# A hybrid attention layer on one core: 72 TensorE transposes become 32x32 block transposes on VectorE, and the planner counts the pieces of transfers under way

## The chip, the core and the metric

The kernel runs on one core of a Trainium2 chip. The metric is the time of the whole program on the device in microseconds. One launch computes everything: a prompt of 1,024 tokens and a sample of 32 tokens, in float32.

The core's engines are TensorE (PE in the profile, with its weight loads as PEld), VectorE (DVE), ScalarE (ACT) and GpSimd (POOL). SyncE (SP) issues all transfers of this kernel, in the order of its instructions.

## The reference

One layer, applied to the prompt and to the sample with the same weights:

```python
hn = rmsnorm(h, g_pre)
qA, kA, vA, gA, qB, kB, vB, gB = split(hn @ w_in)       # eight times 512 columns
oA = band_attention(qA, kA, vA, rel_bias)               # 8 heads x 64, own chunk of 64 and 8 before
oB = stick_breaking(qB, kB, vB)                         # 8 heads x 64, strictly causal
y  = concat(oA * silu(gA), oB * silu(gB)) @ w_out
h  = h + rmsnorm(y, g_post)
h  = h + sigmoid(h @ w_ple_gate) * (p @ w_ple)
```

The sample's 32 queries also attend to 512 cached keys and values for each kind of attention. Besides the two results, the outputs are the new keys and values: those of kind A for the last 512 prompt tokens, those of kind B for all 1,024, and all of them for the 32 sample tokens.

## The kernel before

**Tiles.** The 1,024 + 32 tokens lie side by side as 1,056 columns in three blocks of 352 (`CH`). The normed input is kept transposed, features on the partitions, split into a high and a low float32r half (`hnh`, `hnl`), and every large product is the sum of three float32r products. `norm_tile` scales a tile of 128 tokens (`scale_x`), and `turn_x` transposes it, by eight transposes of 128x128 against the identity on TensorE into PSUM; ScalarE copies the high half from there, VectorE subtracts for the low half.

**Order of the program.** First the tiles of x are loaded, scaled and turned and the first pair's q, k and v are projected, block by block. Then come eight steps, one for each pair of heads, A and B in turn. In a step, `weave` interleaves the attention of this pair (`seq`: scores S, turned weights T, values V for each block of 128 queries) with the projections of the next pair (`den`); `RATE` sets the ratio in which it takes from the two, `SPACE_S`, `SPACE_T` and `SPACE_V` add to the weights of the attention's pieces. In the odd pairs the sample's attention for four heads (`sample_attention`: load, queries, scores, weights, values, out) is inserted at the positions `SAMPLE_AT`. In four steps, sums of quarters of w_out and w_ple_gate are made (`sum_weights`), at fixed positions. After that come the gates' projections, the product of p with w_ple (`class Ple`), and the two 1,024 x 1,024 products by Strassen-like blocks, which end the program.

**The planner.** No engine's order is the program's. `Recorder` records every operation with the operations that it depends on, and its `order` runs a list simulation: each engine has a time at which it is free, each operation a cost (`cost`), and of the operations that are ready the one with the smallest key `(class or low, number in the program)` goes next. A transfer occupies SyncE for `ISSUE` = 550 ns, moves after `DMA_NS` = 1500 ns, at `DMA_RATE` or a cost by pieces, and is taken to have landed `DMA_MARGIN` = 2000 ns later. All instructions come from one line of the recorder, so the profile gives the line 462 for each, and tiles and operations tell them apart.

**Buffers that the change touches.** The tag "tok" of `at2` has two buffers. Keys (`keys_out`), values before and after their turn (`values_out`), p_prompt's tiles (`load_p`) and the left sides of the last products rotate through them. The rings "om" and "be" hold the attention's rows and also tiles of x and the cached keys (`Kc`).

**Transposes before the change, other than the attention's weights.**
- K for its output: VectorE turns the prompt's columns in 32x32 blocks, and four stores, one for each group of 32 features, put them right in pieces of 128 bytes. The 32 sample tokens go through one TensorE transpose (`short_block`) and a copy.
- V, which the attention needs with tokens on the partitions: VectorE turns 32x32 blocks, a store to a scratch and four loads move whole blocks, and ScalarE orders them. The sample tokens go through `short_block` again.
- The sample's cached keys: a load of 128 tokens x 256 features four times, and eight TensorE transposes for each of the four sample attentions.
- The sample's outputs: the diagonal blocks of PSUM are copied to one tile, two TensorE transposes and a copy turn them, and two stores write them.
- p_prompt: two transposes for each tile of 128 tokens.

Of the kernel before, what the change touches and what calls it, by code (L numbers as in the profile page):

```python
# [13 lines left out]
P = 128  # L14
# [12 lines left out]
NT = 9  # L27

# [5 lines left out]
SPACE_S = 0.1  # L34
SPACE_T = 0.4
SPACE_V = 0.0
PARTS = 4
BEHIND = 2
RATE = 1.0
# [135 lines left out]
class Op:  # L175
    __slots__ = ("eng", "what", "args", "kw", "key", "busy", "late", "ready", "left", "after", "at", "size", "shared", "table")
# [7 lines left out]
DMA_NS, DMA_RATE, DMA_MARGIN = 1500, 320.0, 2000  # L184
# [81 lines left out]
class Recorder:  # L266
# [44 lines left out]
    def add(self, eng, what, args, kw):  # L311
# [29 lines left out]
        o.busy, o.late = self.cost(eng, method, args, kw, writes, reads)  # L341
        o.shared = eng == "POOL"
        if eng == "DVE":
            sbuf = [v for v in reads if isinstance(v, (View, Segments)) and not v.buf.psum and v.free() > 4]
            o.shared = len(sbuf) > 1 or (method == "tensor_copy" and len(sbuf) == 1 and not writes[0].buf.psum)

# [35 lines left out]
    def order(self):  # L382
# [16 lines left out]
        out, port, line, table = [], 0.0, 0.0, AF.Exp  # L399
        while len(out) < len(self.ops):  # L400
# [67 lines left out]
def stream_step(  # L468
# [27 lines left out]
    vs_dr = {ab: scratch([NS, 512], f"vs_dr{ab}") for ab in "AB"}  # L496
# [102 lines left out]

    def turn_x(t, sq, n):  # L600
        for kh in range(2):
# [105 lines left out]
    def values_out(ab, p, src, o_p, o_s, then):  # L707
# [5 lines left out]
        def turn():  # L713
# [27 lines left out]
    def col_steps(j):  # L741
# [67 lines left out]
    def attention(ab, p, h):  # L809
# [152 lines left out]
        for i in range(8):  # L962
            out["S", i] = (0.107 * cost(i) + SPACE_S, lambda i=i: scores(i))
            out["T", i] = (0.107 * cost(i) + SPACE_T, lambda i=i: weights_t(i))
        for g in range(2):
            columns = sum(reach(g, b).stop - reach(g, b).start for b in range(4 * g + 4))
            out["V", g] = (0.00088 * columns + SPACE_V, lambda g=g: values(g))
# [11 lines left out]
    def sample_attention(ab, gi):  # L979
# [19 lines left out]
        def queries():  # L999
# [25 lines left out]
        def scores():  # L1025
# [33 lines left out]
            dma(vn, vs_dr[ab][:, 256 * gi:256 * gi + 256])  # L1059
# [33 lines left out]
        def values():  # L1093
# [792 lines left out]
```

## Time and profile before

| | |
|---|---|
| time, median of 3 runs | 786.2 us (785.92 to 786.36) |
| span of the profiled execution | 784.8 us |
| TensorE busy | 776.3 us, 4,606 matmuls, clock 0.999 |
| VectorE, ScalarE, GpSimd busy | 582.2, 531.6, 475.1 us |
| DMA | 153.64 MB in 161,245 packets, of which 38,593 under 512 bytes |

The profile is of one execution; of that execution it gives the span, from its first to its last instruction, and no other time of its own. The span is 1.4 us under the median of the runs, and this difference is carried along. Instructions of an engine are counted busy from start to end, so overlapping matmuls have a longer mean duration than the step from one to the next.

### The profile page before, as it was taken

The page shows a single profiled execution, that of the slowest core. Times are in us where ns is not written, and L with a number is a line of the kernel's source. Part 1 is how long each engine was busy: PE and PEld are TensorE (multiplying, and loading weights), DVE is VectorE, ACT ScalarE, POOL GpSimd, SP SyncE. Part 2 cuts the span into 40 slices and gives each one's busy share as a digit, 9 for nine tenths or more (in the row PEclk, how much of TensorE's full clock was granted, in tenths as well). Part 3 has the DMA queues.
Part 4 walks back from the last instruction along what each step waited for, and adds up shares of the span by engine and source line. Part 5 has one row for each costly group of instructions (what it writes and reads, how often), then busy time and mean ns, then how long its engine had stood idle before and what let it go on. Part 6 is the DMA issues. An engine that isn't in the chain of part 4 may idle for free.

```text
span 784.8 us, 14442 instructions
## 1 busy us (share of the span) xinstructions
PE 776.3 (99%) x4606; PEld 718.1 (92%) x4606; DVE 582.2 (74%) x1106; ACT 531.6 (68%) x1171; POOL 475.1 (61%) x555
## 2 busy tenths in 40 slices
PE   8999999999999999999999999999999999999997
PEld 6999999999999999999999999999998787888786
DVE  7717577896788788786888688766565677989965
ACT  6647686786797677787776697753347967777651
POOL 5626534666585447775966586566553529599523
PEclk9999999999999999999999999999999999999999
DMA  9627634538774638776758767556589856859854
GB/s 304 214 82 190 144 91 133 154 82 257 202 198 138 174 96 248 191 230 190 202 167 244 186 212 236 169 170 186 145 272 309 271 171 204 285 167 342 276 161 134
DMA packets 161245, 153.64 MB, mean 196 GB/s; under 512 B 38593, under 2 KB 127337, under 8 KB 161170
## 3 DMA queue, kind: packets, MB, share of 16 engines
q1 hardware_dynamic: 161170, 152.73, 65.4%
q8 instruction: 36, 0.59, 0.3%
q14 instruction: 39, 0.32, 0.1%
HBM read 94.45 MB, written 49.83 MB: 184 GB/s over the span
## 4 chain that ended last, share of the span: by engine, by line
PE 94%; POOL 2%; DVE 1%; DMA 1%; issue 1%; SPq 0%; ACT 0%; DVEq 0%; ACTq 0%; POOLq 0%
PE mm_kB L462 6%; PE mm_vA L462 6%; PE mm_gA L462 6%; PE mm_qA L462 6%; PE mm_qB L462 6%; PE mm_gB L462 6%; PE mm_vB L462 5%; PE mm_kA L462 5%; PE SB L462 4%; PE PVB L462 4%; PE SA L462 4%; PE PVA L462 3%; PE ptwA L462 3%; PE ptwB L462 3%; PE g1P L462 2%; PE o3P L462 2%
## 5 line engine op out<-in xcount | busy, mean ns | idle before, releaser
L462 POOL TENSOR_TENSOR be<-be,om 128x256 f32<-128x256 f32 (+8 forms) x66 | 85.4, 1298 | 78.6 <-DVE om L462 31.3
L462 DVE TENSOR_TENSOR_SCAN om<-om,SB 128x384 f32<-128x384 f32 (+5 forms) x96 | 92.4, 967 | 20.2 <-ACT be L462 12.4
L462 POOL TENSOR_SCALAR be<-be,statA 128x640 f32<-128x640 f32 (+3 forms) x64 | 45.7, 719 | 44.5 <-DVE statA L462 33.4
L462 ACT ACTIVATE om<-SB 128x384 f32<-128x384 f32 (+5 forms) x96 | 46.8, 497 | 25.7 <-DVE SB L462 19.2
L462 ACT ACTIVATE be<-SB 128x384 f32<-128x384 f32 (+5 forms) x96 | 46.5, 498 | 9.3 <-DVE wTl L462 3.7
L462 ACT ACTIVATE be<-om,statA 128x640 f32<-128x640 f32 (+3 forms) x64 | 44.6, 698 | 11.5 <-DVE statA L462 5.9
L462 DVE TENSOR_TENSOR wTl<-ptwA,wTh 128x512 fp32r<-128x512 f32 (+2 forms) x80 | 37.5, 483 | 14.6 <-ACT wTh L462 13.8
L462 ACT CAST wTh<-ptwA 128x512 fp32r<-128x512 f32 (+2 forms) x80 | 32.6, 425 | 15.1 <-PE ptwA L462 14.1
L462 DVE TENSOR_TENSOR wTl<-ptwB,wTh 128x512 fp32r<-128x512 f32 (+3 forms) x64 | 33.9, 546 | 6.0 <-ACT wTh L462 5.6
L462 DVE CUSTOM_DVE_ANT_0 om<-SA,biasA 128x320 f32<-128x320 f32 (+3 forms) x64 | 30.2, 484 | 6.2 <-PE SA L462 5.5
L462 ACT CAST wTh<-ptwB 128x512 fp32r<-128x512 f32 (+3 forms) x64 | 29.4, 485 | 7.6 <-PE ptwB L462 7.0
L462 PE MATMUL SB<-kdB,LB 128*128 128x384 f32 (+5 forms) x96 | 33.6, 356 | 0.3 <-DVE LB L462 0.3
L462 PE MATMUL ptwA<-ident,be 128*128 128x128 f32 x200 | 33.4, 273 | 0.0
L462 PE MATMUL SB<-klB,LB 128*128 128x384 f32 (+5 forms) x96 | 32.8, 346 | 0.0
L462 DVE TENSOR_TENSOR wTl<-be,wTh 128x640 fp32r<-128x640 f32 (+1 forms) x24 | 29.7, 1237 | 3.2 <-ACT wTh L462 3.1
L462 PE MATMUL SA<-kdA,LA 128*128 128x320 f32 (+2 forms) x96 | 30.6, 322 | 0.0
L462 PE MATMUL SA<-klA,LA 128*128 128x320 f32 (+2 forms) x96 | 30.0, 313 | 0.0
L462 PE MATMUL ptwB<-ident,be 128*128 128x128 f32 x192 | 29.5, 273 | 0.0
L462 POOL TENSOR_TENSOR oB<-oB,oB 128x256 f32<-128x256 f32 x32 | 26.5, 853 | 3.9 <-DMA oB<-in_w_out_dram 3.9
L462 PEld LDWEIGHTS ptwA<-ident,be 128*128 128x128 f32 x200 | 24.8, 140 | 1.1
L462 POOL TENSOR_TENSOR klA<-stkA,kdA 64x1024 fp32r<-64x1024 f32 (+2 forms) x9 | 20.0, 2218 | 9.5 <-ACT kdA L462 9.2
L462 DVE STREAM_TRANSPOSE om<-be 128x640 f32<-128x640 f32 (+1 forms) x24 | 22.2, 925 | 4.6 <-POOL be L462 3.9
(711 smaller groups left out, 2676.7 us busy)
## 6 DMA issues: line engine op xcount, KB each, us to landing
oB<-in_w_out_dram SPq DMA_DIRECT2D x16, 256.0 KB, 4.2
sum_dro<-oB SPq DMA_DIRECT2D x16, 256.0 KB, 2.5
gB<-in_w_ple_gate_dram SPq DMA_DIRECT2D x16, 256.0 KB, 4.2
sum_drg<-gB SPq DMA_DIRECT2D x16, 256.0 KB, 2.3
x<-in_x_prompt_dram SPq DMA_DIRECT2D x16, 256.0 KB, 4.4
h_dr<-h SPq DMA_DIRECT2D x8, 512.0 KB, 4.1
ht<-h_dr SPq DMA_DIRECT2D x8, 512.0 KB, 4.1
raw<-sum_drg SPq DMA_DIRECT2D x16, 256.0 KB, 3.8
```

The source lines that it names most:

```text
L462: getattr(getattr(tc.nc, o.what[0]), o.what[1])(*args, **kw)
```

## The change

Five groups of transposes leave TensorE. Each is now done by VectorE in 32x32 blocks, and the blocks are put in their places by the transfers that are there anyway, or by a new pair of them:
- input tile 6: VectorE turns the blocks into the room of tile 3, one store and four loads bring each block to its place, ScalarE and VectorE make the halves from SBUF (`squares_x`);
- the sample rows of K and V: their 32 columns are turned along with the rest or by an instruction of their own, and four small stores write them (`sample_rows`);
- the cached keys: eight loads in pieces of 128 bytes instead of one, and a transpose in place;
- the sample's outputs: four block transposes straight from PSUM, and four stores;
- p_prompt's tiles 4 to 7: four loads in pieces of 128 bytes, and one block transpose into a second "tok" buffer.

The planner changes too. It counts the pieces of the transfers under way and lets a transfer wait, in its simulation, until no more than `AWAY` = 1900 are; a transfer now starts after `DMA_START` = 1950 ns. The stores of K and V to the outputs get a lower rank (`later`: `low` = 1). `AHEAD_OF` moves the rank of operations that write certain tiles, by engine and name. `RATES`, `SPACE_S`, `SPACE_T`, `SPACE_V`, `SUMS_STEP` and `SAMPLE_AT` become values by step or by kind of attention, and the loads of x tiles 6 to 8 stand ahead of the norms of tiles 6 to 8.

```diff
+AHEAD_OF = {
+    ('ACT', 'L'): 100, ('ACT', 'Qfs'): 50, ('ACT', 'stq'): 400, ('ACT', 'x'): -50,
+    ('DVE', 'Kl'): -100, ('DVE', 'cc'): 200, ('DVE', 'h'): -100, ('DVE', 'sq'): -75,
+    ('SP', 'be'): -50, ('SP', 'biass'): 200, ('SP', 'kd'): 50, ('SP', 'pl'): -25,
+    ('SP', 'ple'): 100, ('SP', 'pp'): -200, ('SP', 'sum'): -400,
+}
...
-SPACE_S = 0.1
-SPACE_T = 0.4
-SPACE_V = 0.0
+SPACE_S = {'A': 0.1, 'B': 0}
+SPACE_T = {'A': 0.4, 'B': 0.4}
+SPACE_V = {'A': 0.05, 'B': 0.0}
-RATE = 1.0
+RATES = (0.96, 0.86, 0.92, 1.0, 1.0, 0.86, 1.12, 0.86)
-DMA_NS, DMA_RATE, DMA_MARGIN = 1500, 320.0, 2000
+DMA_START, DMA_DONE, DMA_RATE, DMA_MARGIN = 1950, 300, 320.0, 2000
+AWAY = 1900
...
+        if eng != "PE" and writes:
+            name = str(writes[0].buf.name)
+            kind = (eng, name[:next((i for i, x in enumerate(name) if x.isdigit() or x in "AB_"), len(name))])
+            o.key = (o.key[0], o.key[1] + AHEAD_OF.get(kind, 0))
...
             elif e == "SP":
+                while away and (away[0][0] <= t or flying + o.pieces > AWAY):
+                    landed, pieces = heapq.heappop(away)
+                    flying -= pieces
+                    t = max(t, landed)
+                o.at = t
                 free[e] = t + o.busy
-                line = max(line, t + o.busy + DMA_NS) + o.late
+                line = max(line, t + DMA_START) + o.late
+                heapq.heappush(away, (line + DMA_DONE, o.pieces))
+                flying += o.pieces
...
+    BY_SQUARES = (6,)
+
+    def squares_x(t, sq):
+
+        swap = scratch([P, D], f"x_dr{t}")
+        raw = x34[0][:, (t - 6) * D:(t - 5) * D]
+        nc.vector.transpose(raw.rearrange("p (g k j) -> p k g j", g=4, j=32), sq.rearrange("p (k g j) -> p k g j", k=KD, j=32))
+        dma(swap, raw)
+        for g in range(4):
+            part = swap[:, g * 256:(g + 1) * 256].rearrange("(c i) x -> i c x", i=32)
+            dma(sq[32 * g:32 * g + 32].rearrange("i (c x) -> i c x", c=4), part)
+        src = sq.rearrange("p (c k j) -> p k c j", c=4, j=32)
+        a = t * P - 2 * CH
+        hi, lo = (x[2][:, :, a:a + P].rearrange("p k (c j) -> p k c j", j=32) for x in (hnh, hnl))
+        nc.scalar.copy(hi, src)
+        nc.vector.tensor_tensor(lo, src, f(hi), ALU.subtract)
...
-    def short_block(src, out, nm):
-        pt = psum("T", nm)
-        nc.tensor.transpose(pt[0:NS, 0:P], src[:, SEQ:T], ident)
-        nc.scalar.copy(out[0:NS, 8, :], pt[0:NS, 0:P])
+    def sample_rows(dst, squares):
+
+        for g in range(4):
+            later(dst[:, 32 * g:32 * g + 32], squares[32 * g:32 * g + 32])
+
+    def later(dst, src):
+
+        was, rec.low = rec.low, 1
+        dma(dst, src)
+        rec.low = was
...
-            x = out.rearrange("p b c -> p (b c)")[:, 0:n]
-            nc.vector.transpose(x, src()[:, SEQ - n:SEQ])
+            x = out.rearrange("p b c -> p (b c)")[:, 0:n + NS]
+            nc.vector.transpose(x, src()[:, SEQ - n:T])
...
-                dma(rows[:, :, q], x[q].rearrange("t (c f) -> t c f", f=32))
-            short_block(src(), out, f"ptk{ab}{p}")
-            dma(o_s[0, 0, :, h2, :].rearrange("p h d -> p (h d)"), out[0:NS, 8, :])
+                later(rows[:, :, q], x[q, 0:n].rearrange("t (c f) -> t c f", f=32))
+            sample_rows(o_s[0, 0, :, h2, :].rearrange("p h d -> p (h d)"), x[:, n:n + NS])
...
-            short_block(st, out, f"ptv{ab}{p}")
+            nc.vector.transpose(out[:, 8, 0:NS], st[:, SEQ:T])
...
-            dma(o_p[0, 0, :, h2, :].rearrange("(b p) h d -> p b (h d)", p=P), out[:, b0:8, :])
-            dma(o_s[0, 0, :, h2, :].rearrange("p h d -> p (h d)"), out[0:NS, 8, :])
+            later(o_p[0, 0, :, h2, :].rearrange("(b p) h d -> p b (h d)", p=P), out[:, b0:8, :])
+            sample_rows(o_s[0, 0, :, h2, :].rearrange("p h d -> p (h d)"), out[:, 8, 0:NS])
...
-            dma(vs_dr[ab][:, p * P:(p + 1) * P], tok[0:NS, 8, :])
+            dma(vs_dr[ab][p], tok[:, 8, 0:NS])
...
-            Kc = ring1.tile([P, 4, 256], "Kc" + nm)
-            dma(Kc, ck[0, 0, :, h4, :].rearrange("(b p) h d -> p b (h d)", p=P))
+            Kc = ring1.tile([P, 2, PAST], "Kc" + nm)
+            for a in range(2):
+                rows = ck[0, 0, :, 4 * gi + 2 * a:4 * gi + 2 * a + 2, :].rearrange("(c j) h d -> j c (h d)", j=32)
+                for g in range(4):
+                    dma(Kc[32 * g:32 * g + 32, a, :].rearrange("j (c f) -> j c f", f=32), rows[:, :, 32 * g:32 * g + 32])
...
-                pt = psum("T", f"ptk{nm}{a}")
-                for b in range(4):
-                    nc.tensor.transpose(pt[:, b * P:(b + 1) * P], bx["Kc"][:, b, a * P:(a + 1) * P], ident)
+                pt = bx["Kc"][:, a, :]
+                nc.vector.transpose(pt, pt)
...
-            diag = bx["diag"] = ring1.tile([P, 256], "diag" + nm)
-            nc.gpsimd.memset(diag, 0.0)
+            diag = bx["diag"] = at.tile([P, 2 * HD], F32, tag="ot", name="diag" + nm, bufs=3)
             for h in range(4):
-                src = acc[h * NS:(h + 1) * NS, h * HD:(h + 1) * HD]
-                (nc.scalar.copy if h % 2 else nc.vector.tensor_copy)(diag[0:NS, h * HD:(h + 1) * HD], src)
+                r = slice(h * NS, (h + 1) * NS)
+                nc.vector.transpose(diag[r, 0:HD], acc[r, h * HD:(h + 1) * HD])
 
         def out():
-            pt = psum("T", f"pto{nm}")
-            diag = bx["diag"]
-            for a in range(2):
-                nc.tensor.transpose(pt[:, a * P:(a + 1) * P], diag[:, a * P:(a + 1) * P], ident)
-            Os = at.tile([P, 2, NS], F32, tag="ot", name="O" + nm, bufs=3)
-            nc.vector.tensor_copy(Os, pt[:, 0:2 * P].rearrange("p (a q) -> p a q", a=2)[:, :, 0:NS])
-            for a in range(2):
-                dma(o_dr[s0 + a][:, SEQ:T], Os[:, a, :])
+            for h in range(4):
+                dst = o_dr[s0 + h // 2][h % 2 * HD:(h % 2 + 1) * HD, SEQ:T]
+                dma(dst.rearrange("(c i) q -> i c q", i=32), bx["diag"][h * NS:(h + 1) * NS, 0:HD].rearrange("i (c q) -> i c q", q=32))
...
+                if not self.early:
+                    rows = src.rearrange("(b j) (k f) -> j k b f", j=32, k=2)
+                    x = pp.rearrange("p b c -> p (b c)")
+                    for g in range(4):
+                        dst = x[32 * g:32 * g + 32].rearrange("j (k b f) -> j k b f", k=2, f=32)
+                        dma(dst, rows[:, :, :, 32 * g:32 * g + 32])
+                    turned = at2.tile([P, 2, 4, P], F32, tag="tok", name=f"ppt{j}", bufs=2)
+                    nc.vector.transpose(turned.rearrange("p k b t -> p (k b t)"), x)
+                    self.pp[j] = turned
+                    return
...
+    SUMS_STEP = {2: [8, 34], 4: [10, 28], 5: [8, 28], 6: [14, 28]}
...
-            out.insert(8 + i * 20, (0.0, lambda w=w, kt=kt: sum_weights(w, kt), None))
+            out.insert(SUMS_STEP[n][i], (0.0, lambda w=w, kt=kt: sum_weights(w, kt), None))
...
-    SAMPLE_AT = [1, 10, 15, 22, 27, 32]
+    SAMPLE_AT = {2: [0, 10, 16, 23, 26, 27], 3: [4, 10, 15, 22, 27, 32], 6: [1, 10, 15, 22, 27, 32], 7: [1, 9, 15, 22, 23, 32]}
...
+            if c:
+                for t in (6, 7, 8):
+                    xs[t] = load_x(t)
```

More of the change, by code (lines that the diff above doesn't have):

```diff
@@ L175 @@
 class Op:
-    __slots__ = ("eng", "what", "args", "kw", "key", "busy", "late", "ready", "left", "after", "at", "size", "shared", "table")
+    __slots__ = ("pieces", "eng", "what", "args", "kw", "key", "busy", "late", "ready", "left", "after", "at", "size", "shared", "table")
 LAND = {"PE": 165, "ACT": 0, "DVE": 0, "POOL": 0, "SP": 0, "CTL": 0}
@@ L345, in add, with pieces @@
             o.shared = len(sbuf) > 1 or (method == "tensor_copy" and len(sbuf) == 1 and not writes[0].buf.psum)
+    @staticmethod
+    def pieces(v):
+        n = 1
+        for x in list(v.shape)[:-1]:
+            n *= x
+        return n if len(v.shape) > 2 or not hasattr(v, "buf") else v.shape[0]
     @staticmethod
@@ L495, in stream_step @@
     r_dr = scratch([8, 768], "r_dr")
[L496 removed]
+    vs_dr = {ab: scratch([4, P, NS], f"vs_dr{ab}") for ab in "AB"}
     ple_dr = scratch([T, D], "ple_dr")
@@ L962, in attention @@
         for i in range(8):
-            out["S", i] = (0.107 * cost(i) + SPACE_S, lambda i=i: scores(i))
-            out["T", i] = (0.107 * cost(i) + SPACE_T, lambda i=i: weights_t(i))
+            out["S", i] = (0.107 * cost(i) + SPACE_S[ab], lambda i=i: scores(i))
+            out["T", i] = (0.107 * cost(i) + SPACE_T[ab], lambda i=i: weights_t(i))
         for g in range(2):
             columns = sum(reach(g, b).stop - reach(g, b).start for b in range(4 * g + 4))
-            out["V", g] = (0.00088 * columns + SPACE_V, lambda g=g: values(g))
+            out["V", g] = (0.00088 * columns + SPACE_V[ab], lambda g=g: values(g))
         return out
@@ L1161, in inputs @@
             m, n = (2, P) if t < 8 else (1, NS)
-            pt = psum("T", f"ptp{t}")
-            for b in range(m):
-                for k in range(2):
-                    nc.tensor.transpose(pt[:, (2 * b + k) * P:(2 * b + k) * P + n], pp[0:n, t % 4 + b, k * P:(k + 1) * P], ident[0:n, 0:n])
-            src = pt.rearrange("p (k t) -> p k t", k=4)[:, 0:2 * m, 0:n]
+            if t in (4, 6):
+                src = pp[:, :, t - 4:t - 2, :].rearrange("p k b t -> p b k t")
+            else:
+                pt = psum("T", f"ptp{t}")
+                for b in range(m):
+                    for k in range(2):
+                        nc.tensor.transpose(pt[:, (2 * b + k) * P:(2 * b + k) * P + n], pp[0:n, t % 4 + b, k * P:(k + 1) * P], ident[0:n, 0:n])
+                src = pt.rearrange("p (k t) -> p k t", k=4)[:, 0:2 * m, 0:n]
             hl = at2.tile([P, 2, 4, P], F32R, tag="stg", name=f"php{t}", bufs=3)
@@ L1290, in weave @@
         while ia < len(att) or idn < len(den):
-            take_a = ia < len(att) and (idn >= len(den) or RATE * pa / ta <= pd / td)
+            take_a = ia < len(att) and (idn >= len(den) or RATES[n] * pa / ta <= pd / td)
             if take_a and att[ia][2] and any(x in prep for x in att[ia][2]):
```

28 lines of the change are left out of this document (18 added, 10 removed).

## The prediction

> **What bounds the kernel now.** I read the page first: the busy shares, the granted clock and the chain that ended last.
>
> ```profile
> span 784.8 us, 14442 instructions
> PE 776.3 (99%) x4606; PEld 718.1 (92%) x4606; DVE 582.2 (74%) x1106; ACT 531.6 (68%) x1171; POOL 475.1 (61%) x555
> PEclk9999999999999999999999999999999999999999
> PE 94%; POOL 2%; DVE 1%; DMA 1%; issue 1%; SPq 0%; ACT 0%; DVEq 0%; ACTq 0%; POOLq 0%
> ```
>
> TensorE is busy for 99% of the span at the full clock, and 94% of the chain is its own instructions, one behind the other. A matmul's shown end is modelled, so I then asked for the busy time stretch by stretch, where a hole would show.
>
> ```profile
> 0.00:20.00 20.00, 17.33 (x87) 14.04 (x88) 14.43 (x21) 12.40 (x23) 11.79 (x26) 1.00 0.90 305
> 20.00:60.00 40.00, 39.65 (x254) 37.84 (x254) 18.47 (x35) 21.85 (x45) 18.85 (x31) 1.00 0.48 149
> 200.00:300.00 100.00, 100.00 (x664) 97.33 (x663) 81.78 (x165) 75.20 (x179) 59.67 (x76) 1.00 0.60 168
> 300.00:400.00 100.00, 99.67 (x642) 96.34 (x641) 80.84 (x167) 76.32 (x174) 72.85 (x92) 1.00 0.73 205
> 400.00:480.00 80.00, 80.00 (x531) 77.53 (x530) 62.55 (x154) 60.22 (x141) 57.65 (x72) 1.00 0.73 211
> 760.00:785.00 25.00, 19.89 (x98) 16.51 (x96) 12.48 (x21) 4.41 (x8) 6.45 (x5) 0.98 0.36 115
> ```
>
> The columns are the stretch, its length, then the busy time of PE, PEld, DVE, ACT and POOL, the clock, the DMA share and GB/s. PE's idle time is 2.67 us in the first 20 us, 0.35 up to 60, 0.33 between 300 and 400, and 5.11 at the end, when the last outputs are finished. Between 200 and 480 us it is idle 0.33 us in all. So PE time that is removed should come off the span nearly whole, and nothing that only relieves another engine or SyncE's queue can earn much.
>
> **What leaves TensorE.** The third view is the groups of PE instructions by form, with two pieces of the timeline.
>
> ```profile
> L462 PE MATMUL ptwA<-ident,be 128*128 128x128 f32 x200 | 33.4, 273 | 0.0
> 204.94 0.60 PE L462 MATMUL ptwA<-ident,be 128*128 128x128 f32 x4
> L462 PE MATMUL ptksA<-ident,be 128*128 128x128 f32 x16 | 2.4, 276 | 0.0
> L462 PE MATMUL ptksB<-ident,be 128*128 128x128 f32 x16 | 2.3, 275 | 0.1
> L462 PE MATMUL ptvB<-ident,stvB 128*32 128x128 f32 x4 | 1.1, 272 | 0.0
> L462 PE MATMUL ptosA<-ident,be 128*128 128x128 f32 x4 | 0.9, 273 | 0.0
> L462 PE MATMUL ptx<-ident,be 128*128 128x128 f32 x64 | 9.6, 274 | 1.7 <-DVE be L462 1.7
> L462 PE MATMUL ptp<-ident,pp 128*128 128x128 f32 x16 | 2.9, 332 | 0.0
> ```
>
> The cached keys lose their 16 + 16 transposes; the samples' outputs lose 8 (two in each of four sample attentions, 4 of them in the ptosA row); the 32 sample rows of K and V lose 16 (one for each of K and V in eight head pairs, 4 of them in the ptvB row); the input tile 6 loses 8 of the 64; p_prompt's tiles 4 to 7 lose 8 of the 16. That is 32 + 8 + 16 + 8 + 8 = 72.
>
> The price of one is not its 273 ns, because transposes overlap. Four in a row last 0.60 us from the first start to the last end; less one duration, three steps take 0.60 - 0.273 = 0.327, so one step is 0.109 us. The group row gives the other bound, 33.4 / 200 = 0.167 us of busy time each, which counts the tails that the next matmul covers. I take 0.109, since PE's queue runs on behind the tails. The short ones have the same duration (272 ns) and get the same price. The sum is 72 x 0.109 = **7.85 us** (12.0 at 0.167).
>
> TensorE: Matmul & The Clock Gate, Part 4, in the Trainium skill puts a transpose in a kernel's context at about 275 ns (bf16); the row's 273 ns agrees as a duration, and by the page as a price the sum would be 19.8 us, which the 0.60 us for four speaks against.
>
> **What it puts on the other engines.**
>
> ```profile
> L462 DVE STREAM_TRANSPOSE ktA<-stkA 128x512 f32<-128x512 f32 x4 | 2.8, 695 | 6.6 <-ACT stkA L462 6.6
> L462 DVE STREAM_TRANSPOSE vxB<-stvB 128x1024 f32<-128x1024 f32 x4 | 4.9, 1236 | 0.0
> L462 DVE TENSOR_TENSOR php<-ptp,php 128x512 fp32r<-128x512 f32 x4 | 2.8, 692 | 1.9 <-ACT php L462 1.9
> L462 DVE TENSOR_TENSOR wTl<-be,wTh 128x640 fp32r<-128x640 f32 x16 | 20.6, 1287 | 2.3 <-ACT wTh L462 2.3
> 558.73 0.23 DVE L462 COPY OsB<-ptosB 128x64 f32<-128x64 f32 x1 [1.00 <-PE ptosB L462]
> 551.32 0.22 DVE L462 COPY be<-PVsB 32x64 f32<-32x64 f32 x1 [0.27 <-ACT be L462]
> L462 ACT COPY ktB<-ptkB 32x128 f32<-32x128 f32 x4 | 1.0, 244 | 0.0
> L462 ACT COPY vtB<-stvB 128x1024 f32<-128x1024 f32 x4 | 4.2, 1062 | 0.0
> ```
>
> VectorE: the keys add 8 transposes of 512 columns, 8 x 0.695 = 5.6 us; tile 6 and the 1,024 columns of p_prompt 1.24 each. From the two transpose rows a column is (1236 - 695) / 512 = 1.06 ns over a fixed 154, so V's eight of 32 columns are 8 x 0.19 = 1.5 and K's 32 further columns 8 x 0.034 = 0.3. The 16 transposes of the samples' outputs at a copy's 0.22 replace 8 such copies and 4 of 0.23: +0.8. The low halves are now made from SBUF, not PSUM: between 692 / 512 = 1.35 and 1287 / 640 = 2.01 ns a column, 0 to 0.34 us for each of twelve: 0 to 4.1. Together **10.7 to 14.8 us** on an engine that has 18.2 + 19.2 + 17.5 = 54.8 us of idle time between 200 and 480 us alone. ScalarE loses 16 copies of 0.244, 3.9 us. I cost all this at nothing: PE's matmuls of the projections cover it, as they do now with DVE at 81%. Without that cover it costs its whole length.
>
> VectorE: DVE Perf Modes, Rules for kernel authors, in the Trainium skill, says the opposite of this change: a 128x128 transpose belongs on TensorE where PSUM will do. By the rows the rule is right in engine time, with 10.7 us or more added for 7.85 saved; it is a rival below.
>
> SyncE: the transfers grow by 96: 48 for the sample rows of K and V (four for one), 28 for the cached keys (eight for one, four times), 8 for the samples' outputs, 4 for their new values, 3 for p_prompt, 5 for tile 6. What many pieces of 128 bytes do to the queue stands here:
>
> ```profile
> 87.05 3.53 SPq L462 DMA_DIRECT2D out_dram<-ktB  x4
> 90.68 1.18 SPq L462 DMA_DIRECT2D wr_qA<-in_w_in_dram  x1
> 185.62 0.38 SPq L462 DMA_DIRECT2D be<-in_cache_a_k_dram  x1
> out_dram<-ktB SPq DMA_DIRECT2D x16, 128.0 KB, 4.0
> out_dram<-ktA SPq DMA_DIRECT2D x16, 64.0 KB, 2.6
> 195.22 0.28 PE L462 MATMUL ptksA<-ident,be 128*128 128x128 f32 x1
> ```
>
> Four stores of K hold SyncE 3.53 us, 0.88 each, and the weights behind them start late. An issue thus costs 0.38 to 0.88 us: 36 to 84 us more on the queue, spread over the span. The place that could feel it is the cached keys: their load is issued at 185.62 and first used at 195.22, 9.6 us later. Eight issues, a landing like ktA's and a transpose take 8 x 0.38 + 2.6 + 0.7 = 6.3, or 8 x 0.88 + 3.3 = 10.3 us: 3.3 early or 0.7 late, at most 2.9 us over four sample attentions. I take nothing: the matmuls that need the keys are ordered by the planner's landing time, and projection matmuls fill PE before them; SAMPLE_AT moves the load relative to this, by a few steps each way. The planner's count of pieces under way adds no instruction; it shifts what is issued first.
>
> The transfer of tile 6 is new on a path that PE waits for:
>
> ```profile
> 31.15 1.40 DVE L462 SCALAR_TENSOR_TENSOR be<-x,rs,gpre 128x512 f32<-128x512 f32 x2
> swapA<-vxA SPq DMA_DIRECT2D x4, 512.0 KB, 4.7
> stvA<-swapA SPq DMA_DIRECT2D x16, 128.0 KB, 3.5
> 51.92 1.46 PE L462 MATMUL mm_kA<-hnh,wh_kA 128*128 128x352 f32 x8
> 560.31 0.60 PE L462 MATMUL ptp<-ident,pp 128*128 128x128 f32 x4
> 596.16 0.71 PE L462 MATMUL ple<-wph0False,php 128*128 128x512 f32 x2
> ```
>
> The tile is scaled by 32.55 us. Transpose 1.24, store 4.7, three more issues at 0.88 = 2.6, reload 3.5, copy 1.06 and low half 2 x 1.03 bring it to 47.7. The third column block, which alone reads it, starts at 51.92, or 51.0 without eight transposes: hidden, with 3.3 us to spare. p_prompt's transposes stand 36 us ahead of the first product, so its four loads are covered by the gate projections. The new keys AHEAD_OF, RATES, SPACE and SUMS_STEP only reorder; with PE full I put them at nothing, from -2.1 (the rival of the start) to the costs in the rivals.
>
> **Sum.** 784.8 - 7.85 = 776.9 us of span. The runs' median, 786.2, stands 1.4 above this profile's span, so the time is **778.3 us**. About 0.2% (1.6 us) is what a measurement of this kernel can tell from no change.
>
> **The rivals.** (a) *The new order also closes PE's early holes.*
>
> ```profile
> 12.37 0.66 PE L462 MATMUL ptx<-ident,be 128*128 128x128 f32 x4 [1.37 <-DVE be L462]
> ```
>
> This wait for the scaled x, with the 0.35 and 0.33 us of the stretches, is about 2.1 us: 776.2. Loads of x get other keys, which speaks for it; that VectorE's work there must wait for x to land speaks against. The 5.11 us of the end stay. (b) *A transpose is worth its whole duration:* 72 x 0.273 = 19.7, 766.5 us. The step of 0.109 is against it. (c) *The small transfers come late:* 2.9 us at the keys, and as much again if tile 6 misses its 3.3 us by that much: 781.2 to 784.1. (d) *PE is not relieved:* the holes stay where the transposes stood, because each waits for the same data by another path; 786.2. Against it: filler matmuls stand between nearly all transposes. (e) *VectorE becomes the bound,* as the rule against the change has it: 14.8 us on the chain less 7.85, 793.2. This begins where its 18% of idle time in the attention stretches is gone; the addition there is about 10 us in 500. (f) *Slower, by the stores that give way.* K's stores hold one of the two "tok" buffers until they land. Put behind all others, they delay the next use, the transpose of V's sample rows at the head of VectorE's queue, with the scans and low halves of the attention behind it, and the values of the next head pair. It decides from 7.85 / 8 = 0.98 us a pair; half a landing of 4.0 us each gives 8 x 2.0 - 7.85 = +8.2, 794.4. Against it: a store goes whenever nothing else is ready, and the planner counts the buffer as a dependency.
>
> **Chances.** Forecast 0.60, (a) 0.13, (b) 0.02, (c) 0.12, (d) 0.03, (e) 0.02, (f) 0.08. Faster by over 0.2% are the forecast, (a), (b) and (c): 0.87; same is (d), 0.03; slower (e) and (f), 0.10. The range takes in the forecast, (a) and most of (c): from 774.2, the sum at 0.167 us each, to 783.0, between the two ends of (c). It leaves out about 0.17.
>
> **What would show it.** In the changed profile: 4,534 PE matmuls; PE busy near 768 us and still 99%; no ptks, ptos, ptk or ptv groups; STREAM_TRANSPOSE groups of 128x512 near 0.7 us; DVE near 595 us; no PE idle of over 0.5 us before the samples' scores or the third column block. A PE share of 98% or less, with idle time ended by DVE or a DMA, would mean (c), (e) or (f); a PE busy time down by much more than 8 us would mean (b).

## The result, and the profile after

The changed kernel takes 783.64 us (median of 7 runs), the kernel before in the same session 785.92: a ratio of 0.9969 (95% interval 0.9958 to 0.9979). It is faster, but by 2.3 us instead of 7.9, and outside the range. All times here are medians; one of the four runs of `t_only`, further down, took 2,687 us, and its ratio leaves that one out. The page of the changed kernel, in the order in which that of before was read:

```profile
span 781.9 us, 14437 instructions
PE 769.8 (98%) x4534; PEld 711.2 (91%) x4534; DVE 602.9 (77%) x1127; ACT 528.4 (68%) x1146; POOL 471.7 (60%) x551
PE 80%; POOL 7%; DVE 4%; DMA 3%; issue 3%; SPq 2%; ACT 1%; POOLq 0%; DVEq 0%; ACTq 0%
```

The 72 matmul instructions are gone, and TensorE is busy 6.5 us less. But the span is only 2.9 us shorter, and the chain that ended last, 94% TensorE before, now passes through GpSimd, VectorE, transfers and issue for a fifth of its length. TensorE has got holes: it is idle for 12.1 us of the span, 8.5 before. The busy time by stretch, after:

```profile
0.00:20.00 20.00, 16.98 (x85) 13.79 (x86) 14.21 (x21) 12.14 (x22) 11.52 (x25) 1.00 0.89 303
200.00:300.00 100.00, 99.59 (x645) 95.95 (x645) 83.84 (x164) 72.64 (x166) 58.18 (x73) 1.00 0.63 169
300.00:400.00 100.00, 99.54 (x637) 95.74 (x636) 80.99 (x169) 74.56 (x168) 70.80 (x90) 1.00 0.72 202
700.00:760.00 60.00, 58.08 (x250) 44.94 (x249) 50.46 (x75) 35.91 (x69) 38.50 (x31) 1.00 0.80 270
```

TensorE's idle time is 3.02 us in the first 20 us, 0.41 and 0.46 in the two stretches of attention, and 1.92 us between 700 and 760, where not one of the moved transposes stood. The two kernels run the same 1,863 operations from the first matmul of the two last products on. Cutting each profile at that matmul (it starts at 609.49 us before, at 604.15 after) gives the shares of the shortfall. First before, then after, columns as in the prediction:

```profile
0.00:609.49 609.49, 605.90 (x3859) 582.54 (x3860) 444.30 (x900) 418.89 (x944) 368.55 (x453) 1.00 0.65 188
609.49:784.80 175.31, 170.40 (x749) 135.56 (x747) 137.88 (x206) 112.74 (x228) 106.53 (x102) 1.00 0.69 224
```

```profile
0.00:604.15 604.15, 598.92 (x3786) 575.76 (x3787) 463.64 (x922) 416.94 (x921) 365.31 (x449) 1.00 0.67 191
604.15:781.90 177.75, 170.89 (x749) 135.40 (x747) 139.29 (x206) 111.49 (x227) 106.40 (x102) 0.99 0.67 221
```

The part with the transposes became 609.49 - 604.15 = 5.3 us shorter; the products, with the same 749 matmuls, became 177.75 - 175.31 = 2.4 us longer. Of the 7.85 us forecast, 2.5 are thus missing before the products and 2.4 in them. What TensorE waited for, before and then after (total us, times, longest):

```profile
PE ptx L462 <- DVE be L462: 1.7, 2, 1.4
PE idle L462 <- DVE newh L462: 1.3, 1, 1.3
PE SB L462 <- DVE LB L462: 0.3, 1, 0.3
```

```profile
PE ptx L490 <- DVE be L490: 1.5, 2, 1.2
PE idle L490 <- DVE newh L490: 1.3, 1, 1.3
PE ptwB L490 <- POOL be L490: 1.0, 2, 0.8
PE g0P L490 <- DVE S2g L490: 1.0, 1, 1.0
PE g1P L490 <- DVE uu L490: 1.0, 1, 1.0
PE ple L490 <- ACT wph0True L490: 0.5, 1, 0.5
...
```

New are the waits for `be` (the attention's rows), for `S2g` and `uu` (both in the last product, 0.97 and 0.95 us) and for the high half of a weight at the start. None is for a transposed tile.

### The profile page after: what moved, and what is told of

Read it like the earlier page. It is cut to its first block, busy times and chain, and to the rows that moved or that the text cites. A ratio compares the mean times of both kernels' runs of the same rounds, so it can differ in the third digit from the quotient of the medians.

```text
span 781.9 us, 14437 instructions
## 1 busy us (share of the span) xinstructions
PE 769.8 (98%) x4534; PEld 711.2 (91%) x4534; DVE 602.9 (77%) x1127; ACT 528.4 (68%) x1146; POOL 471.7 (60%) x551
## 4 chain that ended last, share of the span: by engine, by line
PE 80%; POOL 7%; DVE 4%; DMA 3%; issue 3%; SPq 2%; ACT 1%; POOLq 0%; DVEq 0%; ACTq 0%
PE mm_gB L490 6%; PE mm_qB L490 6%; PE mm_qA L490 5%; PE mm_vA L490 5%; PE mm_kA L490 5%; PE mm_vB L490 5%; PE mm_kB L490 4%; PE PVB L490 4%; PE SB L490 4%; PE PVA L490 3%; PE SA L490 3%; PE ptwA L490 3%; PE o1P L490 3%; PE g2P L490 2%; PE o0P L490 2%
## 5 line engine op out<-in xcount | busy, mean ns | idle before, releaser
L490 POOL TENSOR_TENSOR be<-be,om 128x256 f32<-128x256 f32 (+8 forms) x66 | 83.5, 1269 | 82.1 <-DVE om L490 48.9
L490 POOL TENSOR_SCALAR be<-be,statA 128x640 f32<-128x640 f32 (+4 forms) x64 | 46.0, 727 | 25.8 <-DVE statA L490 22.2
L490 ACT ACTIVATE be<-om,statA 128x640 f32<-128x640 f32 (+4 forms) x64 | 44.4, 695 | 5.9 <-DVE statA L490 3.9
L490 ACT CAST wTh<-ptwB 128x512 fp32r<-128x512 f32 (+3 forms) x64 | 29.8, 488 | 15.4 <-PE ptwB L490 10.7
L490 POOL TENSOR_TENSOR gB<-gB,gB 128x256 f32<-128x256 f32 x32 | 26.0, 821 | 1.5 <-DMA gB<-in_w_ple_gate_dram 1.3
L490 PEld LDWEIGHTS ptwB<-ident,be 128*128 128x128 f32 x192 | 23.0, 140 | 3.1 <-POOL be L490 1.7
```

Source lines behind the costliest of these rows:

```text
L490: getattr(getattr(tc.nc, o.what[0]), o.what[1])(*args, **kw)
```

## The experiments

Three theories stood against each other, and the expectations call them by number. *Theory 1, the new keys:* the new planner and its ranks are worse in themselves. *Theory 2, the moved work:* the 20 us more on VectorE or the 96 transfers more on SyncE delay something. *Theory 3, the order:* the planner's order of either kernel is fitted to its own program, the new one less well; the moved work is hidden. All runs that have `AHEAD_OF`, other than the changed kernel, also break ties of equal rank by the number in the program; `a_kc`, which has this too, keeps the order of the changed kernel's instructions on TensorE and VectorE.

**The price of a transpose.** `twice`: the kernel before in its own order, the 72 transposes issued twice.

```diff
+                    if o.what[1] == "transpose" and o.eng == "PE" and moved(o.args[0].buf.name):
+                        getattr(getattr(tc.nc, o.what[0]), o.what[1])(*args, **kw)
```

> The kernel before with its own order of every engine kept: the 72 transposes that the change moves are each issued twice in place (4,678 matmuls). It prices a transpose on TensorE by itself. With the step of 0.109 us: +7.85 us, 793.8. With 0.167 of busy time: +12.0, 797.9. With PE partly waiting there anyway: under +6, below 792.

Measured: 793.73 us against 786.53, ratio 1.0106 (1.0085 to 1.0126). The span grows from 784.8 to this:

```profile
span 791.4 us, 14586 instructions
PE 784.0 (99%) x4678; PEld 726.3 (92%) x4678; DVE 583.0 (74%) x1106; ACT 531.9 (67%) x1171; POOL 474.2 (60%) x555
```

That is 6.6 us by the spans and 7.2 by the medians, 0.092 to 0.100 us each. The price of 0.109 was a little high, by 0.7 to 1.2 us in all.

**Each half alone.** `t_only` moves the transposes but keeps the old planner and its numbers; `order_only` has the new planner and numbers, with the transposes on TensorE.

```diff
# t_only, against the changed kernel
+AHEAD_OF = {}
+RATES = (1.0,) * 8
...
     def later(dst, src):
-        was, rec.low = rec.low, 1
         dma(dst, src)
-        rec.low = was
# order_only, against the changed kernel
-    BY_SQUARES = (6,)
+    BY_SQUARES = ()
...
-                pt = bx["Kc"][:, a, :]
-                nc.vector.transpose(pt, pt)
+                    nc.tensor.transpose(pt[:, b * P:(b + 1) * P], bx["Kc"][:, b, a * P:(a + 1) * P], ident)
...
```

> The 72 transposes moved, with the planner and its numbers as in the kernel before: no ranks of AHEAD_OF, no count of pieces, no yielding stores, the old ratios and positions, the old places of the loads of x. Theory 1 (the new order opens the holes: the transposes save their 7.85 us, and the ranks, the pieces, the yielding stores and the new ratios give about 5 of it back): 778 to 779.5 us, PE's idle time as before, near 8.5 us. Theory 2 (the moved work itself opens them, by 20 us more on VectorE and 96 more transfers on SyncE): 783 to 787 us, with holes before scores or turned weights in the attention stretches. Theory 3 (any new order shifts holes by a few us, whatever made it new): anything from 778 to 788, and holes at other places than in the changed kernel.

> The other half alone: the transposes stay on TensorE; ranks, count of pieces, yielding stores, ratios, positions and early loads of x are those of the changed kernel. Theory 1: 5 us over the kernel before, 790 to 791.5, with the holes of the changed kernel in the last products (S2g, uu) and the attention. Theory 2: within 1 us of before, 785 to 787. Theory 3: up to 3 us to either side.

Measured: `t_only` 1.0136 (1.0118 to 1.0154), some 11 us, `order_only` 808.21 us, 1.0279 (1.0266 to 1.0293). Both halves are slower than before, and together they are faster. That is no sum of two effects; it suits an order whose numbers fit only the program for which they were chosen. Both lie outside the ranges of all three theories: none had expected so large a spread.

**The ranks.** `no_ahead` empties `AHEAD_OF`; `a_last` takes out only the three ranks that bear on the last products.

```diff
# no_ahead
+AHEAD_OF = {}
# a_last
-    ('DVE', 'Kl'): -100, ('DVE', 'cc'): 200, ('DVE', 'h'): -100, ('DVE', 'sq'): -75,
-    ('SP', 'be'): -50, ('SP', 'biass'): 200, ('SP', 'kd'): 50, ('SP', 'pl'): -25,
+    ('DVE', 'Kl'): -100, ('DVE', 'sq'): -75,
+    ('SP', 'be'): -50, ('SP', 'biass'): 200, ('SP', 'kd'): 50,
```

> The changed kernel with AHEAD_OF empty, all else kept. Theory 1 with the ranks as its main part (they push VectorE's work for cc and pull that for h in the last products, and K's halves in the samples): 779 to 781, without the two holes of 1.1 us at 700 and 710 us. Theory 2: 783 to 785, the holes in the attention stretches still there. Theory 3: 780 to 788, holes elsewhere.

> The changed kernel without the three ranks that act only in the last products (VectorE's cc and h, SyncE's pl); the order up to there is the same. Theory 1 for this place (VectorE takes h ahead of the left side S2g, and PE waits for it): the two holes at 700 and 710 us close, 781 to 782. If the holes come from when the rows and the weights arrive there: 783 to 785.

Measured: `no_ahead` 799.03 us, 1.0162 (1.0148 to 1.0177), 15 us above the changed kernel and outside all three ranges; `a_last` 783.74, 0.9970 (0.9958 to 0.9981), with the holes at `S2g` and `uu` still there (0.9 and 1.4 us). So ranks that add and remove no instruction are worth 15 us, and the holes of the products are not due to these three.

**Without any change of work.** One constant of the planner (`MARGIN`, in ns, added to the time at which TensorE may use a result) is changed: in the kernel before to 410 (`null_b`), in the changed one to 410 (`null_a`) and 390 (`null_a2`).

```diff
-MARGIN = 400
+MARGIN = 410
```

> The kernel before, its work unchanged; only the planner's safety time ahead of TensorE is 410 instead of 400 ns, so the list simulation falls into another order. Theory 3 (the orders of the two kernels fit their programs, and any other order opens holes): 3 to 15 us slower than before, 789 to 801. Theories 1 and 2 (particular keys, or the moved work): within 2 us of before, 784.5 to 788.

> The changed kernel with the same 410 instead of 400 ns. Theory 3: 3 to 15 us over the changed kernel's 783.6, 787 to 799. Theories 1 and 2: within 2 us of it, 782 to 785.5.

> The changed kernel with the planner's safety time ahead of TensorE at 390 instead of 400 ns, by which, unlike with 410, most of PE's order becomes another. Theory 3: 4 to 16 us over the changed kernel, 788 to 800. Theory 2 alone: within 2 us of it.

Measured: `null_b` 793.91 us, 1.0090 (1.0074 to 1.0106); `null_a` 783.70, 0.9960 (0.9944 to 0.9975); `null_a2` 797.27, 1.0159 (1.0138 to 1.0180). `null_b` and `null_a2` are as theory 3 has it. `null_a` misses theory 3's range, but its order hardly moved, so it decides nothing: 4,510 of the 4,534 matmuls stand where they stood, in `null_a2` 2,595. The page of `null_b`:

```profile
span 791.0 us, 14470 instructions
PE 779.8 (99%) x4606; PEld 718.0 (91%) x4606; DVE 582.6 (74%) x1106; ACT 531.8 (67%) x1171; POOL 478.4 (60%) x555
```

The instructions of every engine are those of before; 10 ns in the planner's belief cost 7.4 us, as much as all 72 transposes. The share of 99% doesn't show it, since TensorE has it here too: it is idle for 2.7 us more (11.2 against 8.5), and busy for 3.5 us more with the same 4,606 matmuls.

**The moved work with the order kept.** `dve_twice`: the kernel before in its order, with VectorE's block transposes of K and V issued twice (17 us more, close to the change). `sp_more`: 96 further stores of K and V behind the stores that are there. Then two from the other side, in the order of the changed kernel. `a_kc` loads the cached keys with one transfer instead of eight and turns 32 of their 512 columns; the rest stays unturned, so this kernel leaves out the sample's right results. `a_rows` leaves out three of each four small stores of V's sample rows, and with them these outputs. Its edit doesn't reach the stores of K: SyncE issues 814 transfers there against 838, 24 fewer and not the 48 of its expectation.

```diff
# dve_twice
+                    if o.eng == "DVE" and o.what[1] == "transpose" and o.args[0].buf.name[:2] in ("kt", "vx"):
+                        getattr(getattr(tc.nc, o.what[0]), o.what[1])(*args, **kw)
# sp_more
+                        for _ in range(2 if len(args[1].shape) == 3 and o.args[1].buf.name[0] == "k" else 1):
...
+                            tc.nc.sync.dma_start(to, args[1])
# a_kc
+                if KC and o.eng == "DVE" and name[:2] == "Kc":
+                    tc.nc.vector.transpose(args[0][:, 0:32], args[1][:, 0:32])
+                    continue
...
# a_rows
+                if ROWS and o.eng == "SP" and isinstance(o.args[1], View) and o.args[1].shape == [32, 32] and o.args[1].buf.name[:2] in ("kt", "vt") and o.args[1].box[0][0]:
+                    continue
```

> The kernel before with its order kept: the sixteen block transposes of K and V (kt, vx) are issued twice in place, 4 x 0.70 + 12 x 1.24 = 17.6 us more on VectorE, as much as the change adds (20.7 us busy). Theory 2 with VectorE as the cause: 3 us or more slower, 789 to 800. Theories 1 and 3: VectorE's idle time takes it, 785.5 to 788.

> The kernel before with its order kept: 96 more transfers on SyncE, each right behind a store of K or V, and to scratch: the 32 stores of K in pieces of 128 bytes twice more, the 32 others of the rows of K and V once more. Theory 2 with SyncE's queue as the cause: 3 us or more slower, 789 to 805. Theories 1 and 3: within 2 us, 785 to 788. These copies are larger than what the change adds, so a small rise is no proof for theory 2.

> The changed kernel with its order of every engine kept, and most of the work that the cached keys moved taken away: one transfer loads them instead of eight (28 fewer on SyncE), and VectorE turns 32 of the 512 columns (8 x 0.5 us less); the keys are then not turned, so the sample's results are left out. If the moved work still holds PE up in the changed order (theory 2): 779.5 to 782.5, and the holes at 171 to 174 us are gone. If what is left of the loss is the order alone (theory 3): 783 to 784.5.

> The changed kernel with its order kept, without three of each four small stores of the 32 sample rows of K and V (48 fewer on SyncE); three quarters of those outputs are left out. Theory 2 with SyncE's queue as the cause: 780 to 782.5. Theory 3: 783 to 784.5.

Measured: `dve_twice` 796.96 us, 1.0144 (1.0114 to 1.0174); `sp_more` 806.26, 1.0234 (1.0210 to 1.0258); `a_kc` 783.93, 0.9968 (0.9956 to 0.9981); `a_rows` 783.10, 0.9961 (0.9949 to 0.9974). The first two alone speak for theory 2: `dve_twice` lies in its range, `sp_more` just above it. But their work is work that the order doesn't know of, and such work is dear. `a_kc` and `a_rows`, which take away work that the order does know of, gain nothing clear of the noise, as theory 3 has it; TensorE's wait of 0.8 us for `be` near 174 us is still there in `a_kc`. The largest hole of `dve_twice` shows how the price arises, behind two lines of the kernel before (timeline; start, us):

```profile
379.07 0.86 DVE L462 TENSOR_TENSOR v2B<-vtB,v2B 128x512 fp32r<-128x512 f32 x1
379.35 2.82 POOL L462 TENSOR_TENSOR be<-be,om 128x1024 f32<-128x1024 f32 x2
```

```profile
383.72 1.43 PE L462 MATMUL mm_qA<-hnh,wh_qA 128*128 128x352 f32 x8
388.26 0.27 PE L462 MATMUL ptkA<-ident,stkA 128*32 128x128 f32 x1 [3.11 <-DVE wTl L462]
383.11 0.71 DVE L464 STREAM_TRANSPOSE ktA<-stkA 128x512 f32<-128x512 f32 x1
383.75 3.76 DVE L462 TENSOR_TENSOR v2B<-vtB,v2B 128x512 fp32r<-128x512 f32 x1
383.38 2.36 POOL L462 TENSOR_TENSOR be<-be,om 128x1024 f32<-128x1024 f32 x2
385.71 2.93 POOL L462 TENSOR_TENSOR wl_vA<-wr_vA,wh_vA 128x512 fp32r<-128x512 f32 x2
```

The transpose issued twice costs 0.7 us. In the kernel before, the subtraction for `v2B` starts 0.28 us ahead of a pair of GpSimd additions and lasts 0.86 us. Now it starts 0.37 us behind them and lasts 3.76 us, and TensorE, in its fixed order, stands for 3.1 of the 9.5 us by which the span grew. In `sp_more` one hole of the same length goes back to a load:

```profile
210.15 1.65 SPq L467 DMA_DIRECT2D copy<-ktB  x2
211.91 0.40 SPq L462 DMA_DIRECT2D be<-in_cache_a_v_dram  x1
216.19 0.43 DVE L462 CAST Vh0sA<-be 128x512 fp32r<-128x512 f32 x1 [4.01 <-DMA be<-in_cache_a_v_dram]
218.00 1.44 PE L462 MATMUL PVA<-wTl,v2A 128*128 128x512 f32 x4 [3.07 <-DVE wTl L462]
```

The load of the cached values is issued behind the copies, at 211.91 us instead of the 202.66 of the kernel before; VectorE waits 4.01 us at their first use, with the low halves of the weights behind it.

**An order fitted anew.** The theory of the order says that numbers searched again for a program bring its holes back down. `fit_a1` and `fit_a2` are the changed work with ranks, rates and positions searched against the planner's own simulation, for other safety times; `fit_o3` is the program of `order_only`, its numbers searched likewise.

```diff
# fit_a2 (fit_a1 and fit_o3 in the same places)
-    ('DVE', 'Kl'): -100, ('DVE', 'cc'): 200, ('DVE', 'h'): -100, ('DVE', 'sq'): -75,
+    ('DVE', 'Kl'): -50, ('DVE', 'cc'): 175, ('DVE', 'h'): -625, ('DVE', 'sq'): -325,
...
-RATES = (0.96, 0.86, 0.92, 1.0, 1.0, 0.86, 1.12, 0.86)
+RATES = (0.95, 0.92, 0.92, 0.94, 0.88, 0.95, 1.25, 0.81)
-MARGIN = 400
-ISSUE = 550
+MARGIN = 500
+ISSUE = 500
...
```

> The changed kernel's work in a third order: the safety time ahead of TensorE is 390 ns, by which alone the order fell to 797.3 us, and the numbers AHEAD_OF, RATES, SPACE, SUMS_STEP and SAMPLE_AT are searched anew until the planner's list simulation ends as early as with the changed kernel's own numbers. If an order must be fitted to its program and any fitted one will do (theory 3), it comes back to the changed kernel's time, 781 to 786. If the changed kernel's order was an unlucky fit, 778 to 781. If the search fits the planner and not the chip, 787 to 797.

> The same work, searched anew under longer safety times: 500 ns ahead of TensorE, 2400 instead of 2000 ns after a transfer. Theory 3 with the planner's times as the gap (TensorE's order counts on data that the chip brings later): fewer holes than in the changed kernel, 777.5 to 781. If the moved work itself holds TensorE up, whatever the order: 782.5 to 785.

> The transposes back on TensorE, the order's numbers searched anew for this program (with the changed kernel's numbers it took 808.2 us). Theory 3: the time of the kernel before, 785 to 788.5, since both halves then have an order of their own. Theory 1 (the new planner and its ranks are worse in themselves): 790 or more. Its distance to fit_a1 is the price of the 72 transposes with the order's luck evened out: 7 us if the moved work is free, 3 if it is not.

Measured: 782.37 us, 0.9954 (0.9940 to 0.9969); 781.66, 0.9945 (0.9931 to 0.9959); 789.91, 1.0046 (1.0034 to 1.0058). `fit_o3` gains 18 us on `order_only` by numbers alone. Between fitted orders of both programs, 789.91 and 782.37, lie 7.5 us, about the price of the transposes. But fitted orders of one program differ too: `fit_o3` and the kernel before, both with the transposes on TensorE, by some 4 us. Only `fit_a1` lies in theory 3's range. `fit_a2` falls between the two ranges of its expectation, and `fit_o3` is 1.4 us above theory 3's, next to the 790 of theory 1; by itself it doesn't exclude that the new planner is a little worse.

**The order of the last stage alone.** `graft_a` is the changed kernel with the order of the products' 1,863 operations taken from the kernel before; `graft_b` the reverse, `graft_best` is `fit_a2` with that stage from before (a few operations fewer in both). `TAIL` gives the place of each operation in the other order.

```diff
+TAIL = (
...
+)
-        return out
+        return out[:8112] + [out[8112 + i] for i in TAIL]
```

> The changed kernel; only the order of the two products that end the program (1,863 operations, the same ones in both kernels, no transpose that moved among them) is taken from the kernel before. From the first o0P matmul to the last matmul of the program the kernel before takes 170.1 us, the changed one 172.5. Theory (the shortfall is the planner's order, here in a stage that the transposes don't touch): the holes before g0P and g1P go, 783.6 - 2.4 = 781.2 us. Rival (TensorE, relieved, arrives 5.3 us early and finds the other engines and loads not further on, whatever the order): the holes stay, 783.6.

> The kernel before; only the order of those 1,863 operations at the end is taken from the changed kernel. Theory (order): 786.0 + 2.4 = 788.4 us, with holes before g0P and g1P. Rival (an early TensorE makes the holes): 786.0, no holes.

> The changed work with the numbers of fit_a2 up to the products, and the order of the kernel before from there. In fit_a2 the products start at 602.3 us and take 172.4. Theory (order): 602.3 + 170.1 + 5.2 to the end of the span + 1.8 = 779.4 us, faster than all so far. Rival (an early TensorE, here by 7.2 us, makes the holes): 781.7 or more.

Measured: 780.83 us, 0.9926 (0.9913 to 0.9938); 789.14, 1.0029 (1.0018 to 1.0040); 779.51, 0.9907 (0.9892 to 0.9922). The stage, cut at its first matmul, in `graft_a`, `graft_b` and `graft_best`:

```profile
604.06:779.40 175.34, 170.40 (x749) 135.56 (x747) 137.99 (x206) 112.87 (x228) 106.68 (x102) 0.99 0.68 224
```

```profile
610.07:787.70 177.63, 170.86 (x749) 135.33 (x747) 139.45 (x206) 112.00 (x227) 106.51 (x102) 1.00 0.67 221
```

```profile
0.00:602.48 602.48, 598.15 (x3786) 576.53 (x3787) 458.11 (x921) 415.18 (x919) 367.06 (x449) 1.00 0.68 192
602.48:777.80 175.32, 170.40 (x749) 135.57 (x747) 137.71 (x206) 112.63 (x228) 106.54 (x102) 1.00 0.69 224
```

The order takes its 2.4 us along to whichever kernel it is put in, so a TensorE that arrives early is not the cause. The two holes go along as well. `graft_a` and `graft_best` have neither; `graft_b` has both:

```profile
PE g0P L559 <- DVE S2g L559: 1.1, 1, 1.1
PE g1P L559 <- DVE uu L559: 0.9, 1, 0.9
```

TensorE's own order in the products is the same in both kernels; the orders of VectorE, ScalarE and GpSimd differ. The timeline names the place, in the changed kernel first and then in `graft_a`:

```profile
698.89 1.71 DVE L490 TENSOR_TENSOR gT<-raw,gT 128x512 fp32r<-128x512 f32 x1
701.12 0.67 DVE L490 TENSOR_TENSOR S2g<-xS2g,S2g 128x512 fp32r<-128x512 f32 x1
701.85 2.57 PE L490 MATMUL g0P<-gT,S2g 128*128 128x512 f32 x10 [0.97 <-DVE S2g L490]
```

```profile
697.31 1.72 DVE L587 TENSOR_TENSOR gT<-raw,gT 128x512 fp32r<-128x512 f32 x1
699.54 0.68 DVE L587 TENSOR_TENSOR S2g<-xS2g,S2g 128x512 fp32r<-128x512 f32 x1
700.21 2.92 PE L587 MATMUL g0P<-gT,S2g 128*128 128x512 f32 x12
```

VectorE does the same subtractions, 1.6 us earlier, and no gap is left. `graft_best` is the fastest kernel of the study. Up to the products it gains 609.49 - 602.48 = 7.0 us on the kernel before, the whole measured price of the transposes, with the moved work in place. That work isn't quite free there: one wait of TensorE, 0.7 us, is for the turned outputs of a sample attention (`diagsA`).

## Why the prediction was wrong

**The step that failed** is "the new keys AHEAD_OF, RATES, SPACE and SUMS_STEP only reorder; with PE full I put them at nothing". TensorE was full in the order of the kernel before, and that order was replaced, not kept; `null_b` shows that another order of the same instructions can cost 7.4 us. The changed kernel's own order costs 2.4 us in the products (`graft_a`, `graft_b`) and, before them, 7.0 - 5.3 = 1.7 us more than the best order found for the same work (`graft_best`). That is 4.1 of the 7.85 - 2.9 = 4.95 us of span that are missing. The 1.7 is a difference of single executions, and the spans of the changed kernel's seven runs go from 780.7 to 782.8; the medians of `graft_a` and `graft_best`, which differ in nothing but the order before the products, give 1.3 us. The upper end of the range, 783.0, was priced at late transfers; orders of the changed kernel's work spread from 779.5 (`graft_best`) to 799.0 us (`no_ahead`).

**The transposes' price,** 7.85 us, was mis-sized by little: 6.6 to 7.2 where they are added. That is about the rest. Rival (b), 19.7 us, is refuted by `twice`.

**VectorE's new work at nothing** nearly holds where the order counts it (`graft_best`, with its wait of 0.7 us). Its price per instruction was near:

```profile
L490 DVE STREAM_TRANSPOSE be<-be 128x512 f32<-128x512 f32 x8 | 5.6, 700 | 0.0
L490 DVE STREAM_TRANSPOSE diagsA<-PVsA 32x64 f32<-32x64 f32 x8 | 2.0, 245 | 0.7 <-PE PVsA L490 0.6
L490 DVE TENSOR_TENSOR Kl0sB<-be,Kh0sB 128x512 fp32r<-128x512 f32 x2 | 2.5, 1270 | 0.0
L490 DVE STREAM_TRANSPOSE vtA<-stvA 128x32 f32<-128x32 f32 x4 | 0.8, 192 | 0.0
L490 DVE TENSOR_TENSOR v2B<-vtB,v2B 128x512 fp32r<-128x512 f32 x8 | 8.2, 1050 | 2.0 <-ACT v2B L490 2.0
```

The total was not: VectorE's busy time grew by 602.9 - 582.2 = 20.7 us, not 10.7 to 14.8. Added up over the groups by form (number times mean), the instructions that the change adds or replaces make 13.6 us, inside the forecast; those that it leaves alone, such as `v2B`, make 7.5 more, since they lasted longer where they now stand. In `fit_a2` VectorE is busy for 594.9 us, inside the forecast. The reason given for the cover was wrong, though: idle time of VectorE in a stretch. `dve_twice` had all of it and lost 10 us.

**SyncE's 96 transfers at nothing** is supported by `a_kc` for the keys and by `a_rows` for V's sample rows; K's were not taken away by themselves. That all 96 together cost little is shown by `graft_best`, which has them. Here too `sp_more` shows that this was the order's merit, not the queue's room.

**Tile 6** came when it was forecast: ready at 46.19 + 1.47 = 47.66 us (47.7), its first reader at 51.00 (51.0). That it is so exact is luck. The tile was scaled 0.65 us later than before, and its reload, issued at 37.54, could be read at 45.10, 1.5 us more than its two terms of 2.6 and 3.5; the store, with its reload issued 3.0 us behind it instead of 4.7, and the low half, 1.47 instead of 2.06, took less.

```profile
46.19 1.47 DVE L490 TENSOR_TENSOR hnl<-be,hnh 128x1024 fp32r<-128x1024 f32 x1 [2.81 <-ACT hnh L490]
51.00 1.46 PE L490 MATMUL mm_kA<-hnh,wh_kA 128*128 128x352 f32 x8
```

**The other rivals.** (a) fell: the wait for the scaled x is 1.2 us instead of 1.4, and the first 20 us have more idle time, not less. (c) has the measured time between its ends, 781.2 and 784.1, but not its reason: TensorE waits for no transferred key, tile 6 was on time, and `a_kc` gains nothing. (d) and (e) fell: TensorE is relieved, VectorE is at 77%. (f) fell: V's transpose waits for no store (0.0 us of idle time in the rows of `vtA` and `vtB`). The sign named in advance, a share of 98% with idle time ended by VectorE, did appear, but it meant none of these: the prediction had no rival in which the order alone leaves holes.

**Open** is what in the planner puts the products in the worse order; the three ranks of `a_last` don't. Also not settled is where each of the 1.7 us before the products goes; `graft_best` shows only that the moved work doesn't force them.

## What to carry to other kernels

In a kernel whose engines follow an order that was fitted beforehand, a share of 99% on one engine doesn't tell that the order is as good as it can be, nor that there is room beside it. Work moved off the full engine is gained in full only if the new order fits as well as the old one, and a change of the order's numbers has to be priced as a term of its own, here by several microseconds of either sign. Measure that spread first, by changing a constant that alters no instruction. Then cut both profiles at the same instruction: a stage that became longer with the same work in it points at the order, and exchanging the order of that stage alone, in both directions, tests it.

## What the runs showed of the hardware

A subtraction on VectorE has no fixed length. The low half of the cached keys took 677 ns with one operand in PSUM (before); with both in SBUF it took this in `fit_a2`, against 1,270 ns in the changed kernel:

```profile
L493 DVE TENSOR_TENSOR Kl0sB<-be,Kh0sB 128x512 fp32r<-128x512 f32 x2 | 1.3, 656 | 0.0
```

So the source alone costs nothing; what runs beside it can, as with the `v2B` of 0.86 us before and 3.76 us in `dve_twice`. SBUF — State Buffer, Who interferes with whom, in the Trainium skill says that a VectorE instruction with two SBUF inputs contends with a GpSimd instruction that reads SBUF. The same page of the Trainium skill, in its Summary: rules for kernel authors, says that of these two the second to issue waits until the first has finished. The rows agree with the first part: the long `v2B` lies beside additions of GpSimd. They don't show how long one blocks the other: the 3.76 us, from 383.75 to 387.51, run past both additions of `be`, which end at 385.74, and into the pair behind them.
